# The sums of W_s over q: VectorE and a way through HBM in place of two products with ones

## The chip, the core and the metric

The kernel runs on one core of a Trainium2 chip. The metric is the device time of one execution in microseconds (us), the median of several runs. The core's engines work side by side, each through its own queue, and wait for one another by semaphores: TensorE (PE) multiplies, VectorE (DVE) and ScalarE (ACT) work elementwise, GpSimd (POOL) does small things and issues some transfers, and SyncE (SP) issues most of the transfers.

## What is computed

One layer of an encoder over 1024 positions of 1024 features. Of its parts, the spatial gate matters here:

```python
def spatial_gating(u, v, w_s, b_s, ln_g, ln_b):
    v = layer_norm(v, ln_g, ln_b)
    vc = v.reshape(bsz, s // CHUNK, CHUNK, N_HEADS_A, HEAD_DIM_A)
    mixed = jnp.einsum('hpq,bcqhd->bcphd', w_s, vc) + b_s.T[None, None, :, :, None]
    return u * mixed.reshape(bsz, s, D_A)

h = rms_norm(x, pre_g)
u_a, v_a, g_a, z_b, g_b = jnp.split(h @ w_in, ...)
a = spatial_gating(gelu(u_a), gelu(v_a), w_s, b_s, ln_g, ln_b) * silu(g_a)
b = fourier_mix(z_b, w_f, b_f) * silu(g_b)
x = x + rms_norm(concat([a, b]) @ w_out, post_g)
```

W_s is 128x128 for each of four heads. The layer norm's bias ln_b is constant over positions, so its way through the gate is ln_b times the sum of W_s over q, for each head and each p.

## The kernel before

The x is held transposed, features on partitions. Every product that needs float32 is made of three products of rounded halves (mm3, L75 to L78): high by high, high by low, low by high. A helper split (L68 to L73) makes the two halves of a matrix: a cast on ACT and a subtraction on DVE.

The order of PE's work is written out by hand. First the product for v: seven of eight chunks of positions side by side over the eight blocks of features (L234 to L241), then the eighth (L251 to L253). Meanwhile stats (L152) makes the row norms of x: squares on ACT, a power on POOL (rsqrt, L97), then the 1024 factors go to HBM (r_hbm, L159) and come back broadcast to all partitions as R (L160), both on POOL's queue. v_gelu (L169) and v_norm (L175) turn the product into the normalised v, without ln_g and ln_b. In v_norm an rsqrt on POOL stands between two small operations on DVE, and the norms themselves run on ACT.

Then feature_tile (L388) runs for the twelve tiles of 128 features, in two halves of 512 positions each; with the halves numbered through, after(i) (L458) hangs other work behind half i. Behind half 2 stands gate_bias (L376), then gate_head for the first head (L424), whose products take v and the transposed W_s (ws_sb); the other heads follow behind halves 4, 6 and 8. z_fold, z_step, wz_load and the weights of later tiles (feature_load, which ends in the splits such as wf2h and wf2l) lie between. gate_bias adds ln_b times the row sums of W_s into Tb, which holds b_s broadcast; gate_head reads Tb on DVE only.

Before the change the row sums come from PE. W_s lies transposed in ws_sb, q on partitions, so two products with a matrix of rounded ones, of the high half and of the low half (row_sum, L142 to L144), leave the sums in every partition of a PSUM bank (pt). The split of ws_sb into wss (L384, L385) stands ahead of the feature tiles. The rounded ones (ones_r) are made by ACT as its first operation (L93).

PE, and ACT inside one stretch (L242 to L255), keep the written order; POOL and DVE do so only late, from the last four feature tiles on. Elsewhere a planner orders each engine by its own costs: what is ready and stands first in the program goes first. The planner also hands out the 40 big buffers (slot, L57), and a load waits in SP's queue until its buffer is free.

Of the kernel before, what the change touches and what calls it, by code (L numbers as in the profile page):

```python
# [7 lines left out]
F32 = mybir.dt.float32  # L8
F32R = mybir.dt.float32r
AF = mybir.ActivationFunctionType  # L10
ALU = mybir.AluOpType
PE = mybir.EngineType.PE

P = 128
S = 1024
# [15 lines left out]
def encoder_layer_kernel(  # L31
# [6 lines left out]
    w_fea: bass.AP,  # L38
    w_out: bass.AP,
    w_sT: bass.AP,  # L40
    w_f: bass.AP,
    b_s: bass.AP,
    post_g: bass.AP,
# [3 lines left out]
    nc = tc.nc  # L47

    big = ctx.enter_context(tc.tile_pool(name="big", bufs=1))
    con = ctx.enter_context(tc.tile_pool(name="con", bufs=1))  # L50
# [6 lines left out]
    def slot(name, shape=(P, 1024), dt=F32):  # L57
        return big.tile(list(shape), dt, tag="S", name=name, bufs=NS)
# [6 lines left out]
    def bank(name):  # L65
        return ps.tile([P, 512], F32, tag="ps", name=name)

    def split(src, hi, lo, hi_on_act=True):  # L68
        if hi_on_act:
            nc.scalar.copy(hi, src)  # L70
        else:
            nc.vector.tensor_copy(hi, src)
        nc.vector.tensor_tensor(lo, src, hi.bitcast(F32), op=ALU.subtract)  # L73
# [14 lines left out]
    pre_g, ln_g, b_f, ln_b = (vec_sb[:, a:b] for a, b in ((0, 8), (8, 12), (12, 16), (16, 20)))  # L88

    ones = con.tile([P, P], F32, name="ones")  # L90
    nc.vector.memset(ones, 1.0)
    ones_r = con.tile([P, P], F32R, name="ones_r")
    nc.scalar.copy(ones_r, ones)  # L93
    expo = con.tile([P, 8], F32, name="expo")
    nc.gpsimd.memset(expo, -0.5)

    def rsqrt(dst, src):  # L97
        nc.gpsimd.tensor_tensor(dst, src, expo[:, 0:src.shape[1]], op=ALU.pow)
# [13 lines left out]
    for kt in range(KT):  # L112
# [13 lines left out]
        h = slot(f"hh{kt}", dt=F32R)  # L126
# [12 lines left out]
    def chunk(t, c):  # L139
        return t[:, c * P:(c + 1) * P]  # L140

    def row_sum(o, hi, lo, sl):  # L142
        nc.tensor.matmul(o, ones_r, hi[:, sl], start=True, stop=False)
        nc.tensor.matmul(o, ones_r, lo[:, sl], start=False, stop=True)  # L144


    rcol = con.tile([P, 8], F32, name="rcol")
    msq = con.tile([P, 8], F32, name="msq")
    R = slot("R")
    r_hbm = ctx.enter_context(tc.tile_pool(name="hbm", bufs=1, space=bass.MemoryType.DRAM)).tile([1, S], F32, name="r_hbm")  # L150

    def stats():  # L152
        for c in range(8):
            xc = raw_slot(f"xc{c}")
            nc.sync.dma_start(xc, x[c * P:(c + 1) * P])
            nc.scalar.activation(xc, xc, AF.Square, accum_out=msq[:, c:c + 1])
        nc.vector.tensor_scalar(msq, msq, 1.0 / D, EPS, op0=ALU.mult, op1=ALU.add)
        rsqrt(rcol, msq)
        nc.gpsimd.dma_start(r_hbm.rearrange("o (c p) -> p (o c)", c=8), rcol)  # L159
        nc.gpsimd.dma_start(R, r_hbm.broadcast_to([P, S]))  # L160
# [8 lines left out]
    def v_gelu(c, pv):  # L169
        nc.scalar.activation(v[:, c], pv, AF.Gelu, scale=rcol[:, c:c + 1])  # L170
        nc.vector.bn_stats(vst[:, c], v[:, c])
        nc.vector.bn_aggr(vmv[:, c], vst[:, c])


    def v_norm(c0, c1):  # L175
        nc.vector.tensor_scalar_add(vnb[:, c0:c1], vmv[:, c0:c1, 1], EPS)
        rsqrt(vrs[:, c0:c1], vnb[:, c0:c1])
        nc.vector.scalar_tensor_tensor(vnb[:, c0:c1], vmv[:, c0:c1, 0], -1.0, vrs[:, c0:c1], op0=ALU.mult, op1=ALU.mult)
        for c in range(c0, c1):
            nc.scalar.activation(v[:, c], v[:, c], AF.Identity, scale=vrs[:, c:c + 1], bias=vnb[:, c:c + 1])  # L180

    def v_step(pv, c, kt):
        wh, wl = (t[:, kt % 2] for t in wv[kt // 2])
        mm3(pv, chunk(hh[kt], c), chunk(hl[kt], c), wh, wl, kt == 0, kt == KT - 1)
# [6 lines left out]
    def wz_load(i):  # L191
        wr = raw_slot(f"wz{i}")
        wrv = wr.rearrange("p (k n) -> p k n", k=2)
        nc.sync.dma_start(wrv, w_nat[0, 2 * i:2 * i + 2].rearrange("k p n -> p k n"))
        fw = tmp(f"fw{i}", (P, 2, 512))
        w4 = wrv.rearrange("p k (g c) -> p k g c", g=4)
        e4 = fw[:, :, 0:260].rearrange("p k (g c) -> p k g c", g=4)
        o4 = fw[:, :, 260:512].rearrange("p k (g c) -> p k g c", g=4)
        a, b = w4[:, :, :, 1:64], w4[:, :, :, 127:64:-1]
        nc.vector.tensor_tensor(e4[:, :, :, 1:64], a, b, op=ALU.add)  # L200
        nc.vector.tensor_tensor(o4, a, b, op=ALU.subtract)
        nc.vector.tensor_copy(e4[:, :, :, 0:65:64], w4[:, :, :, 0:65:64])
        for k in range(2):
            kt = 2 * i + k
            h5 = h512[:, kt:kt + 1]
            nc.vector.tensor_tensor(h5, hh[kt].bitcast(F32)[:, 512:513], hl[kt].bitcast(F32)[:, 512:513], op=ALU.add)
            if kt == 0:
                nc.vector.tensor_scalar_mul(acc, fw[:, k, 0:260], h5)
            else:
                nc.vector.scalar_tensor_tensor(acc, fw[:, k, 0:260], h5, acc, op0=ALU.mult, op1=ALU.add)  # L210
        t = slot(f"wzh{i}", (P, 2, 512), F32R), slot(f"wzl{i}", (P, 2, 512), F32R)
        split(fw, *t)
        wz.append(t)

    wsTb = slot("wsTb", (P, 2, 512))
    ws_sb, Tb = wsTb[:, 0], wsTb[:, 1]
# [3 lines left out]
    def const_load():  # L220
        nc.sync.dma_start(ws_sb, w_sT)
        nc.sync.dma_start(Tb, b_s.broadcast_to([P, 512]))
        nc.sync.dma_start(cs_sb, dft[:, 780:909])
        nc.sync.dma_start(wf_sb, w_f)

    def feature_load(f):
        wr = raw_slot(f"wf{f}r")
        nc.sync.dma_start(wr, w_fea[f])
        wh = slot(f"wf{f}h", dt=F32R)
        wl = slot(f"wf{f}l", dt=F32R)  # L230
        split(wr, wh, wl)
        return wh, wl
# [9 lines left out]
    with tc.manual_schedule(engines={mybir.EngineType.Activation}):  # L242
        stats()
        wq = [feature_load(0)]
        wz_load(0)
        const_load()
        for c in range(7):
            v_gelu(c, pvs[c])
        wq.append(feature_load(1))
        v_norm(0, 7)  # L250
        pv = bank("pv7")  # L251
        for kt in range(KT):
            v_step(pv, 7, kt)  # L253
        v_gelu(7, pv)
        v_norm(7, 8)  # L255
# [119 lines left out]

    def gate_bias():  # L376

        pt = bank("pt")
        row_sum(pt, wss[:, 0], wss[:, 1], slice(0, 512))
        for hd in range(4):  # L380
            sl = slice(hd * P, (hd + 1) * P)
            nc.vector.scalar_tensor_tensor(Tb[:, sl], pt[:, sl], ln_b[:, hd:hd + 1], Tb[:, sl], op0=ALU.mult, op1=ALU.add)

    wss = slot("wss", (P, 2, 512), F32R)  # L384
    split(ws_sb, wss[:, 0], wss[:, 1])  # L385


    def feature_tile(f, epilogue):  # L388
# [69 lines left out]
    def after(i):  # L458
        if i == gate_at[0]:
            gate_bias()  # L460
        for kt in range(KT):
            if FOLD_AT[kt] == i:
                z_fold(kt)
        for j in range(2):
            if WZ_AT[j] == i:
                wz_load(2 + j)
        if i in gate_at:
            gate_head(gate_at.index(i))
        if i in z_at:
            kt = z_at.index(i)  # L470
            z_step(kt)
        if i == 9:
            nc.sync.dma_start(dft_sb, dft[:, 0:780])
            channel_split()
        if i == z_at[-1]:
            channel_dft()
            z_evac()
        if i in DFT_AT:
            dft_group(DFT_AT.index(i))
        if i == 22:  # L480
            for _ in range(2):
                next(ahead)
# [198 lines left out]
    lo, hi = slice(0, 512), slice(512, 1024)  # L681
    cuts = (0, 256), (256, 512)
    at = {}
    for n, (g, key) in enumerate(ORDER):
        a, b = 2 * g, 2 * g + 1
        op = ops.pop((g, key))
# [123 lines left out]
```

## Time and profile before

| | us |
|---|---|
| time, median of 3 runs | 311.56 (311.33 to 311.60) |
| the profiled execution | 311.69 |
| its span | 309.6 |
| PE busy | 302.5 (98%) |
| DVE busy | 228.1 (74%) |
| ACT busy | 131.4 (42%) |
| POOL busy | 22.9 (7%) |

The span runs from the first to the last instruction of one profiled execution; the 2.09 us between span and time lie around it. Matmuls are pipelined: a matmul's row shows longer than the step from its start to the next one's start.

### The profile page before, as it was taken

Reading aid. Unit: us, or ns where it says so; the run is one execution under the profiler, and the core shown is the slowest. Engines: PE = TensorE matmul, PEld = TensorE weight load, DVE = VectorE, ACT = ScalarE, POOL = GpSimd, SP = SyncE. Lnnn points to the kernel's source line nnn. Section 1 sums busy time; section 2 is a strip of 40 time slices with the busy share of each in tenths; the row PEclk is TensorE's granted clock in tenths of the full one; section 3 lists DMA queues with packets and bytes.
Section 4 is the critical chain, followed back from the end, with each engine's and each line's share of the span. In section 5 each row is a group of like instructions: output and inputs, shape, how many; then the busy total and the mean of one; then the engine's idle time right before and its main releaser. Section 6 shows DMA issues by size and latency. Waiting matters only on the chain.

```text
span 309.6 us, 3974 instructions
## 1 busy us (share of the span) xinstructions
PE 302.5 (98%) x1497; PEld 254.4 (82%) x1497; DVE 228.1 (74%) x424; ACT 131.4 (42%) x215; POOL 22.9 (7%) x29
## 2 busy tenths in 40 slices
PE   8999999999999999999999999999999999999992
PEld 7888888888888888888888888888888888888881
DVE  4880643579888999987446798655898998898764
ACT  4887376423131333243241334433555554433321
POOL 0000301010000000000000000002300302030210
PEclk9999999999999999999999999999999999999998
DMA  7999715013214252130010107328990163749373
GB/s 252 414 406 409 260 68 177 30 68 128 78 59 147 68 202 56 68 128 10 0 69 2 68 0 233 109 68 243 223 214 1 18 119 67 204 70 276 131 197 144
DMA packets 15427, 42.42 MB, mean 137 GB/s; under 512 B 1456, under 2 KB 1712, under 8 KB 15408
## 3 DMA queue, kind: packets, MB, share of 16 engines
q1 hardware_dynamic: 12880, 35.87, 32.6%
q0 software_dynamic: 2528, 6.30, 11.4%
q8 instruction: 12, 0.20, 0.3%
q14 instruction: 7, 0.06, 0.1%
HBM read 37.96 MB, written 4.20 MB: 136 GB/s over the span
## 4 chain that ended last, share of the span: by engine, by line
PE 98%; DVE 0%; DVEq 0%; POOLq 0%; ACT 0%; issue 0%; ACTq 0%
PE pf L77 14%; PE pf L76 14%; PE pf L78 14%; PE pz L285 7%; PE pv L78 4%; PE pv L77 4%; PE pv L76 4%; PE bb L76 4%; PE bb L78 4%; PE bb L77 4%; PE bc L78 2%; PE bc L77 2%; PE bc L76 2%; PE pg L431 2%; PE ba L76 2%; PE ba L78 2%
## 5 line engine op out<-in xcount | busy, mean ns | idle before, releaser
L446 DVE TENSOR_TENSOR t<-pf,R 128x512 f32<-128x512 f32 x16 | 11.0, 686 | 15.8 <-PE pf L78 15.8
L78 PE MATMUL pv<-wvh,hl 128*128 128x512 f32 x57 | 22.5, 395 | 0.0
L447 ACT ACTIVATE t<-t 128x512 f32<-128x512 f32 x16 | 10.1, 631 | 29.2 <-DVE t L446 29.2
L77 PE MATMUL pv<-wvl,hh 128*128 128x512 f32 x57 | 22.5, 394 | 0.0
L70 ACT CAST fh<-sd 128x1024 fp32r<-128x1024 f32 x8 | 8.4, 1049 | 33.1 <-DVE sd L273 33.1
L76 PE MATMUL pv<-wvh,hh 128*128 128x512 f32 x57 | 22.4, 393 | 0.0
L528 POOL DMA_DIRECT2D wo<-in_w_out x6 | 7.2, 1210 | 175.2 <-PE pf L78 150.3
L285 PE MATMUL pz<-wzh,fh 128*128 128x260 f32 x64 | 18.1, 283 | 0.0
L285 PE MATMUL pz<-wzh,fl 128*128 128x260 f32 x64 | 18.0, 281 | 0.0
L285 PE MATMUL pz<-wzl,fh 128*128 128x260 f32 x64 | 18.0, 281 | 0.0
L562 ACT CAST cq<-s 128x512 fp32r<-128x512 f32 x16 | 9.9, 619 | 17.0 <-DVE s L554 15.3
L644 ACT ACTIVATE jk<-y 128x512 f32<-128x512 f32 x12 | 7.6, 632 | 18.6 <-DVE y L717 7.0
L271 DVE TENSOR_TENSOR sd<-hs 128x384 f32<-128x384 f32 x16 | 14.5, 909 | 0.2
L73 DVE TENSOR_TENSOR fl<-sd,fh 128x1024 fp32r<-128x1024 f32 x8 | 9.8, 1223 | 5.2 <-ACT fh L70 5.1
L77 PEld LDWEIGHTS pv<-wvl,hh 128*128 128x128 f32 x57 | 10.7, 188 | 2.6
L76 PEld LDWEIGHTS pv<-wvh,hh 128*128 128x128 f32 x57 | 10.7, 188 | 2.5
L440 ACT ACTIVATE mixA<-t 128x512 f32<-128x512 f32 x8 | 5.1, 632 | 18.1 <-DVE t L439 18.1
L78 PEld LDWEIGHTS pv<-wvh,hl 128*128 128x128 f32 x57 | 10.7, 187 | 2.5
L439 DVE TENSOR_TENSOR t<-pf,R 128x512 f32<-128x512 f32 x8 | 5.5, 690 | 9.5 <-PE pf L78 9.5
L285 PEld LDWEIGHTS pz<-wzl,fh 128*128 128x128 f32 x64 | 12.1, 189 | 0.3
L285 PEld LDWEIGHTS pz<-wzh,fh 128*128 128x128 f32 x64 | 12.1, 189 | 0.3
L285 PEld LDWEIGHTS pz<-wzh,fl 128*128 128x128 f32 x64 | 12.1, 189 | 0.0
(381 smaller groups left out, 939.5 us busy)
## 6 DMA issues: line engine op xcount, KB each, us to landing
wo<-in_w_out SPq DMA_DIRECT2D x10, 512.0 KB, 4.5
xc<-in_x SPq DMA_DIRECT2D x8, 512.0 KB, 10.0
xr<-in_xT SPq DMA_DIRECT2D x7, 512.0 KB, 7.6
hs<-in_xT SPq DMA_DIRECT2D x7, 512.0 KB, 3.3
wo<-in_w_out POOLq DMA_DIRECT2D x6, 512.0 KB, 9.3
y<-in_x POOLq DMA_DIRECT2D x5, 512.0 KB, 5.2
out<-y SPq DMA_DIRECT2D x5, 512.0 KB, 3.0
wv<-in_w_nat SPq DMA_DIRECT2D x8, 256.0 KB, 6.8
```

What stands on the lines that cost most here:

```text
L70: nc.scalar.copy(hi, src)
L73: nc.vector.tensor_tensor(lo, src, hi.bitcast(F32), op=ALU.subtract)
L76: nc.tensor.matmul(o, lh, rh, start=start, stop=False, **kw)
L77: nc.tensor.matmul(o, lh, rl, start=False, stop=False, **kw)
L78: nc.tensor.matmul(o, ll, rh, start=False, stop=stop, **kw)
L271: nc.vector.tensor_tensor(sd[:, i, 1:4], hv[:, 1:4], hv[:, 7:4:-1, ::-1], op=op)
L285: nc.tensor.matmul(pz[t][:, cs], l[:, i, t], r[:, cs], start=kt == 0 and i == 0 and j == 0, stop=kt == KT - 1 and i == 1 and j == 2, skip_ ...
L446: nc.vector.tensor_tensor(t, pf, R[:, sl], op=ALU.mult)
L447: nc.scalar.activation(t, t, AF.Silu)
L528: nc.gpsimd.dma_start(t, quarter(add, i), accum_op=ALU.add)
L562: nc.scalar.copy(t[:, 0], src)
L644: nc.scalar.activation(jk[:, 0:w], src, AF.Square, accum_out=ssq[c][:, j:j + 1])
```

## The change

W_s comes in a second time in its own order, p on partitions and q along the row, as a new input w_s (128x512, the four heads side by side). It lands in ws_n, one half of a big buffer (wsnr). One tensor_reduce on DVE sums each head's 128 columns into ws_sum (128x4). Its 512 numbers go to HBM (s_hbm) by a transfer on POOL's queue, and a second transfer on POOL's queue broadcasts them to all partitions as ws_row, the other half of the buffer. This is issued behind feature_load(1) and ahead of v_norm(0, 7). gate_bias reads ws_row in place of pt. The two products, the bank pt, the split wss and ones_r are gone.

```diff
     ones = con.tile([P, P], F32, name="ones")
     nc.vector.memset(ones, 1.0)
-    ones_r = con.tile([P, P], F32R, name="ones_r")
-    nc.scalar.copy(ones_r, ones)
...
-    def row_sum(o, hi, lo, sl):
-        nc.tensor.matmul(o, ones_r, hi[:, sl], start=True, stop=False)
-        nc.tensor.matmul(o, ones_r, lo[:, sl], start=False, stop=True)
-
...
         wq.append(feature_load(1))
+
+        wsnr = slot("wsnr", (P, 2, 512))
+        ws_n, ws_row = wsnr[:, 0], wsnr[:, 1]
+        ws_sum = con.tile([P, 4], F32, name="ws_sum")
+        s_hbm = hbm.tile([1, 512], F32, name="s_hbm")
+        nc.sync.dma_start(ws_n, w_s)
+        nc.vector.tensor_reduce(ws_sum, ws_n.rearrange("p (h q) -> p h q", h=4), axis=mybir.AxisListType.X, op=ALU.add)
+        nc.gpsimd.dma_start(s_hbm.rearrange("o (h p) -> p (o h)", h=4), ws_sum)
+        nc.gpsimd.dma_start(ws_row, s_hbm.broadcast_to([P, 512]))
         v_norm(0, 7)
...
     def gate_bias():
 
-        pt = bank("pt")
-        row_sum(pt, wss[:, 0], wss[:, 1], slice(0, 512))
         for hd in range(4):
             sl = slice(hd * P, (hd + 1) * P)
-            nc.vector.scalar_tensor_tensor(Tb[:, sl], pt[:, sl], ln_b[:, hd:hd + 1], Tb[:, sl], op0=ALU.mult, op1=ALU.add)
-
-    wss = slot("wss", (P, 2, 512), F32R)
-    split(ws_sb, wss[:, 0], wss[:, 1])
+            nc.vector.scalar_tensor_tensor(Tb[:, sl], ws_row[:, sl], ln_b[:, hd:hd + 1], Tb[:, sl], op0=ALU.mult, op1=ALU.add)
...
         "w_sT": a["w_s"][0].transpose(2, 0, 1).reshape(128, 512),
+        "w_s": a["w_s"][0].transpose(1, 0, 2).reshape(128, 512),
```

## Rows read from the trace of the kernel before

**Rows 1.** The page: busy us by engine; DVE's busy tenths in 40 slices.

```profile
PE 302.5 (98%) x1497; PEld 254.4 (82%) x1497; DVE 228.1 (74%) x424; ACT 131.4 (42%) x215; POOL 22.9 (7%) x29
...
DVE  4880643579888999987446798655898998898764
```

**Rows 2.** The page: the chain that ended last, share of the span by engine.

```profile
PE 98%; DVE 0%; DVEq 0%; POOLq 0%; ACT 0%; issue 0%; ACTq 0%
```

**Rows 3.** Stretches: length, busy us by engine (PE, PEld, DVE, ACT, POOL), PEclk, DMA.

```profile
77.60:303.70 226.10, 225.96 (x1153) 190.87 (x1151) 180.40 (x335) 85.94 (x151) 16.20 (x18) 1.00 0.39 107
303.70:309.60 5.90, 0.00 (x0) 0.00 (x0) 2.02 (x5) 0.43 (x2) 0.54 (x1) 0.81 0.42 164
```

**Rows 4.** Timeline of PE: start us, us, line, out<-in, count.

```profile
66.93 0.40 PE L143 MATMUL pt<-wss,ones_r 128*128 128x512 f32 x1
...
67.39 1.95 PE L431 MATMUL pg<-wsTb,v 128*128 128x128 f32 x16
...
78.05 0.39 PE L78 MATMUL pf<-hh,wf2l 128*128 128x512 f32 x1
```

**Rows 5.** Timeline of DVE, 59 to 78 us: start, us, operation [idle before, releaser].

```profile
59.19 0.69 DVE L171 BATCH_NORM_STATS2 vst<-v 128x6 f32<-128x512 f32 x1
...
63.42 0.68 DVE L73 TENSOR_TENSOR wss<-wsTb,wss 128x512 fp32r<-128x512 f32 x1
...
70.06 1.13 DVE L382 SCALAR_TENSOR_TENSOR wsTb<-pt,head,wsTb 128x128 f32<-128x128 f32 x4
...
75.55 1.22 DVE L73 TENSOR_TENSOR wf2l<-wf2r,wf2h 128x1024 fp32r<-128x1024 f32 x1
76.68 1.28 DVE L267 SCALAR_TENSOR_TENSOR hs<-hs,head,R 128x1024 f32<-128x1024 f32 x1
```

**Rows 6.** SP's queue: an issue (start, us), and a wait (total, times, longest us).

```profile
48.84 0.33 SPq L266 DMA_DIRECT2D hs<-in_x  x1
...
SPq L266 <- PE pv L77: 17.0, 1, 17.0
```

**Rows 7.** DMA issues: queue, count, KB each, us from issue to landing.

```profile
wsTb<-in_w_sT SPq DMA_DIRECT2D x1, 256.0 KB, 9.6
...
wz<-in_w_nat SPq DMA_DIRECT2D x1, 512.0 KB, 11.7
...
r_hbm<-rcol POOLq DMA_DIRECT2D x1, 4.0 KB, 8.5
...
R<-r_hbm POOLq DMA_DIRECT2D x1, 512.0 KB, 4.0
```

**Rows 8.** Timelines of POOL (three rows) and DVE (the last), 34 to 50 us.

```profile
34.02 1.12 POOL L159 DMA_DIRECT2D r_hbm<-rcol  x1 [0.32 <-POOL rcol L98]
42.78 0.58 POOL L160 DMA_DIRECT2D R<-r_hbm  x1 [7.65 <-DMA r_hbm<-rcol]
47.88 1.51 POOL L98 TENSOR_TENSOR vrs<-vnb,expo 128x7 f32<-128x7 f32 x1 [4.51 <-DVE vnb L176]
...
42.79 1.29 DVE L171 BATCH_NORM_STATS2 vst<-v 128x6 f32<-128x512 f32 x2 [4.70 <-ACT v L170]
```

**Rows 9.** Timeline of ACT: the norms of v, chunks 0 to 6 and 7.

```profile
49.69 5.05 ACT L180 ACTIVATE v<-v,vnb,vrs 128x512 f32<-128x512 f32 x7 [2.53 <-DVE vnb L178]
...
64.81 0.82 ACT L180 ACTIVATE v<-v,vnb,vrs 128x512 f32<-128x512 f32 x1 [1.90 <-DVE vnb L178]
```

**Rows 10.** Timelines of ACT's start and its Gelu table, and PE's first product.

```profile
0.74 1.28 ACT L93 ACT_TABLE_LOAD   x1 [0.74 <-PEq L803]
...
2.94 0.51 ACT L134 ACTIVATE hh<-head 128x256 fp32r<-128x256 f32 x1 [0.61 <-DMA head<-in_x]
...
40.78 1.28 ACT L170 ACT_TABLE_LOAD   x1 [3.94 <-PE pv L78]
...
4.49 1.20 PE L238 MATMUL pv<-wvh,hh 128*128 128x512 f32 x2
```

More of the change, by code (lines that the diff above doesn't have):

```diff
@@ L40, in encoder_layer_kernel @@
     w_sT: bass.AP,
+    w_s: bass.AP,
     w_f: bass.AP,
@@ L149, in encoder_layer_kernel @@
     R = slot("R")
-    r_hbm = ctx.enter_context(tc.tile_pool(name="hbm", bufs=1, space=bass.MemoryType.DRAM)).tile([1, S], F32, name="r_hbm")
+    hbm = ctx.enter_context(tc.tile_pool(name="hbm", bufs=1, space=bass.MemoryType.DRAM))
+    r_hbm = hbm.tile([1, S], F32, name="r_hbm")
     def stats():
```

## Prediction

> **What bounds the kernel now.** I read the page's busy table and slices first, then the chain of waits, then the table by stretches, then TensorE's timeline round the two products that go, and last the engines and queues that the new path will use. The reader is to see in the page [rows 1] that TensorE (PE) is busy 302.5 of 309.6 us and in the chain [rows 2] that 98% of what ended last is PE. The table by stretches [rows 3] makes it sharper: from 77.60 to 303.70 there are 225.96 us of matmuls in 226.10 us, at full granted clock, and the last matmul is followed by a tail of 5.90 us. So PE never waits after its start, and an edit counts by two things alone: how much matmul time it takes away, and whether it makes any operand late. VectorE (DVE) is busy 74% on average, but nine tenths and more in the tenth slice (69.7 to 77.4), right after the edit [rows 1], so an operand from it can easily be late.
>
> The profiled execution took 311.69 us, a span of 309.60 and 2.09 around it. The median shown is 311.56, 0.13 less; I make the sum against 311.69 and take 0.13 off at the end.
>
> **What is removed from PE.** The first of the two products with ones starts at 66.93, and the gate's first product follows them at 67.39 [rows 4]. Starts count, since matmuls overlap: 67.39 - 66.93 = 0.46 us. As nothing but PE is late anywhere behind [rows 2, 3], the whole 0.46 comes off the end. This is the only gain on the path.
>
> **What is removed elsewhere.** The split of the transposed W_s goes: a cast on ScalarE (ACT) and a subtraction of 0.68 us on DVE at 63.42 [rows 5]; also the rounding of ones on ACT at the start. None is on the chain [rows 2], so they are worth nothing to the end; the 0.68 is room for DVE in a stretch where it has little.
>
> **What is added.** One load of 256 KB on SP's queue; one tensor_reduce over 128x512; a write of 512 single floats to HBM and a broadcast of 256 KB back, both on POOL's queue. The four additions into Tb now read SBUF and wait for that broadcast instead of PE.
> - The load stands between those of wf1r and of the second wz in program order. SP was through with wz at 31.8, since the hs load that went at 48.84 had waited 17.0 us by then [rows 6]; so I put the new load at about 31. The load of W_s transposed, as large and in the same stretch, took 9.6 us to land and that wz 11.7 [rows 7]: it lands at 41 to 43. What stands behind it on SP is wz and the hs loads, none of which PE waits for [rows 2], and hs doesn't go before 48.84 for want of a buffer anyway: cost nothing.
> - tensor_reduce isn't in the trace. Its nearest rows are statistics of as many columns, 0.69 us, and a subtraction, 0.68 [rows 5]; from below, half of an operation over 1024 columns of 1.28 [rows 5], 0.64. I take 0.68. DVE stands idle for 4.70 us up to 42.79 [rows 8], and there it costs nothing; at the upper end of its landing it delays the statistics behind it by 0.7 to 1, which the slack worked out below covers. If the planner orders it between 56 and 76 it takes the place of the subtraction that went, 0.68 for 0.68.
> - The write of 512 floats is half of the r_hbm write of 1024, which took 1.12 us of POOL [rows 8] and 8.5 us to land [rows 7]. For the new write I take 8.5 as the upper and the 4.0 of the broadcast R [rows 7] as the lower end, and work with 8.5, because the form is that of r_hbm. POOL is busy with R until 43.36 [rows 8], so the write is issued at 43.4 and has landed at 51.9; ws_row is issued then and lands 4.0 later, at 55.9. The additions run at 70.06 today [rows 5]: 14 us to spare.
> - The four additions take 1.13 us together from PSUM [rows 5]. From SBUF the nearest row is again the 1.28 over 1024 columns: an eighth of it, 0.16 each, from below, and all of it from above would be absurd for 128 columns; the 0.28 each of today is nearest in shape. Not on the path.
>
> The Trainium skill, "DMA: Bandwidth & Descriptors", section "Anatomy of one DMA — SWDGE (gpsimd) path", puts the fixed cost of such a transfer at about 2.0 us. By it the write would land 6.5 us sooner and rival 1 below would keep 2.4 of its 8.9 us of lateness (an estimate from that page); the trace's 8.5 us disagrees and decides.
>
> **What is queued behind the new waits.** On POOL the issue of ws_row waits for the write to land. Behind it, if the planner keeps program order, stands the rsqrt of the norm of v, at 47.88 now [rows 8]; it would run at 51.9 + 0.58 = 52.5. Who waits: the norm of seven chunks on ACT, 5.05 us from 49.69 [rows 9]; then gelu of the eighth chunk, 0.7 like one norm, to 55.4; then its statistics on DVE at 59.19 [rows 5], which leaves 3.8 us of slack; and then the last norm on ACT, which ends at 65.63 [rows 9]. The gate's eighth product needs that at 66.93 + 7 x 0.12 = 67.8 after the change (1.95 us for sixteen, [rows 4]), which leaves 2.1 more. So the rsqrt may be some 5.9 us late, at 53.8, before PE notices, and 52.5 fits. On DVE the additions hold up what follows them in order: wf2l ends at 76.77 [rows 5] and a matmul needs it at 78.05 [rows 4], 1.3 us of slack.
>
> **Buffers.** The raw tile takes one of the 40 big buffers at about 31 instead of the split tile at about 60. The hs load waited 17.0 us for one [rows 6]. If the new load takes the last free buffer, wz goes at 48.84 instead and lands 4.0 later, and hs behind it. PE waits for neither today [rows 2]; I cost it at nothing, and if that cover is gone it is rival 4.
>
> **Sum.** 311.69 - 0.46 = 311.23 for the profiled execution, 311.10 against the median: 0.15% less. About 0.2%, 0.62 us, is what a measurement of this kernel can tell from no change, so the forecast lies within it.
>
> **Rivals.**
> 1. *The detour is late and POOL stands still (slower).* If the load of W_s is the one that gets no buffer, it goes at 48.84, lands 4.0 later at 52.8, is summed at 53.6, the write lands at 62.1, and only then ws_row is issued. If the planner put that issue ahead of the rsqrt, the latter moves from 47.88 to 62.7. ACT norms from 64.5 to 69.5, gelu 0.7, statistics 0.7, rsqrt to norm 1.8 and the norm 0.8 as now [rows 5, 8, 9]: 73.5 instead of the 67.8 at which PE wants it. PE stalls 5.7: 311.56 - 0.46 + 5.7 = 316.8. It decides from an rsqrt later than 53.8. For it: the 17.0 us wait for a buffer and the 8.5 us landing; against it: the load stands ahead of wz and hs in program order, and wz did get a buffer. Chance 0.08.
> 2. *The planner's order shifts on DVE (slower).* DVE's order is the planner's; the additions are free to move ahead and the sum is new. If sum and additions, 0.68 + 1.13, come in front of wf2l, 0.5 of the 1.81 goes beyond its slack and eats the gain: 311.6. If the scaling of hs behind it, 1.28 at 76.68 [rows 5], changes places with it as well, 1.8 of stall: 312.9. I take the middle, 312.3. For it: DVE full there [rows 1] and a slack of 1.3 us; against it: 0.68 went from the same stretch. Chance 0.14.
> 3. *The table load at the start waits.* The first table load of ACT ran at 0.74 with the rounding of ones; it will now belong to the first cast of hh, which waits for its DMA until 2.94 [rows 10]. The load of the Gelu table began only when the wait for PE was over [rows 10]. If so here, 2.94 + 1.28 + 0.51 = 4.73 instead of 3.45, and the first matmul that needs it moves from 4.49 to about 4.8: 0.3 back, 311.4. Against it: the first table load was held by the start alone, not by the memset that its cast needed. Chance 0.10.
> 4. *Nothing comes off.* The 0.46 could be given back in front of some later operand, all of whose slacks I haven't read: 311.6. Chance 0.08.
>
> **How the numbers follow.** Forecast 0.60, rivals 0.08, 0.14, 0.10, 0.08. Predicted is the forecast's 311.1. Its own range is 310.8 to 311.4 (the runs shown differ by 0.27 us). The range to 312.6 takes in rivals 3, 4 and the better half of rival 2, and leaves out 0.15: rival 1 and the worse half. Faster by over 0.2% needs 0.16 us beyond the 0.46: I give it 0.20, from the forecast alone. Within 0.2%: the rest of the forecast, 0.40, and rivals 3 and 4, 0.18, together 0.58. Slower by over 0.2%: rivals 1 and 2, 0.22.
>
> **What would show it.** Right: the gate's first product one matmul step behind the feature tile's last, where three lie now, PE without idle time, and the last matmul 0.46 sooner. The sum on DVE before 44 and ws_row landed before 60 show the detour's step; an rsqrt later than 53.8 or a PE wait at the gate shows rival 1; a PE wait on wf2l rival 2; a table load at 2.9 rival 3. A gain of over 1 us would mean that PE had losses I didn't see.

## The result, and the profile after

The changed kernel takes 318.62 us (median of 5 runs, 318.45 to 318.98) beside 311.60 for the kernel before on the same chip: a ratio of 1.0233, 95% interval 1.0222 to 1.0244, so it is slower by 7.0 us. The prediction was 311.1 with a range to 312.6. The profiled execution took 318.56, with a span of 316.6 against 309.6; the whole loss lies inside the span.

The page of the changed kernel, its busy times, the granted clock of PE in 40 slices and the chain that ended last:

```profile
PE 305.4 (96%) x1495; PEld 256.2 (81%) x1495; DVE 227.9 (72%) x424; ACT 130.9 (41%) x213; POOL 23.9 (8%) x31
...
PEclk9999999999699999999999999999999999999998
...
PE 90%; DMA 4%; DVE 3%; issue 0%; DVEq 0%; POOLq 0%; ACT 0%; ACTq 0%
PE pf L77 12%; PE pf L79 12%; PE pf L78 12%; PE pz L290 8%; PE pv L79 4%; PE pv L78 4%; PE pv L77 4%; PE bb L77 4%; PE bb L78 4%; PE bb L79 3%; DMA s_hbm<-ws_sum 3%; PE bc L77 2%; PE bc L78 2%; PE bc L79 2%; PE ba L78 2%; PE ba L77 2%
```

Beside [rows 1, 2]: PE is busy longer with two products fewer, its clock has a dent in one slice, and DMA and DVE have come into the chain, DMA with the write of the sums (s_hbm<-ws_sum). PE waits in three new places behind the first tile: for v at the gate, and for fh and fl at the first z product. (z_fold scales and folds a block of x and splits it into fh and fl; z_step multiplies these.) PE's timeline, and two rows of the kernel before:

```profile
66.86 1.72 PE L431 MATMUL pg<-wsTb,v 128*128 128x128 f32 x14
69.56 0.49 PE L431 MATMUL pg<-wsTb,v 128*128 128x128 f32 x2 [0.98 <-ACT v L176]
...
78.04 0.59 PE L290 MATMUL pz<-wzh,fh 128*128 128x260 f32 x1 [2.43 <-ACT fh L71]
...
79.41 0.58 PE L290 MATMUL pz<-wzh,fl 128*128 128x260 f32 x1 [0.57 <-DVE fl L74]
...
84.31 0.63 PE L77 MATMUL pf<-hh,wf2h 128*128 128x512 f32 x1
...
85.03 0.40 PE L79 MATMUL pf<-hh,wf2l 128*128 128x512 f32 x1
```

```profile
74.74 0.28 PE L285 MATMUL pz<-wzh,fh 128*128 128x260 f32 x1
...
77.59 0.39 PE L76 MATMUL pf<-hh,wf2h 128*128 128x512 f32 x1
```

The gate starts at 66.86 instead of 67.39 [rows 4]: the two products are gone, as predicted. The first z product, at 74.74 before, starts at 78.04; the third feature tile, at 77.59 before, at 84.31; and its first product with wf2l at 85.03 instead of 78.05 [rows 4]. From there on the lateness stays at 7.0 to the end. The stretches (length; busy us of PE, PEld, DVE, ACT, POOL; granted clock) show that the last part is not waiting alone:

```profile
75.60:78.00 2.40, 0.01 (x1) 0.00 (x0) 2.40 (x7) 1.06 (x2) 0.00 (x0) 1.00 0.09 14
78.00:79.40 1.40, 0.80 (x2) 0.50 (x2) 1.40 (x3) 0.94 (x1) 0.00 (x0) 0.51 0.85 322
79.40:82.00 2.60, 2.59 (x12) 2.59 (x13) 2.60 (x4) 0.63 (x1) 0.00 (x0) 0.50 0.56 224
82.00:84.30 2.30, 2.30 (x12) 2.30 (x12) 2.27 (x3) 0.00 (x0) 0.00 (x0) 0.50 0.00 0
84.30:86.00 1.70, 1.70 (x8) 1.37 (x8) 1.68 (x6) 0.00 (x0) 0.00 (x0) 0.83 0.00 0
```

PE stood idle for 2.4 us and was then granted half its clock, the lower of its two levels, up to 84.3: the 24 products of the first z_step took 6.27 us (78.04 to 84.31) instead of 2.85.

What came late is read off DVE and POOL (start, us; in brackets the idle time before and what ended it), with the fold and an rsqrt of the kernel before behind them:

```profile
56.53 0.68 DVE L252 TENSOR_REDUCE ws_sum<-wsnr 128x4 f32<-128x512 f32 x1
...
68.44 0.16 DVE L174 SCALAR_TENSOR_TENSOR vnb<-vmv,vrs 128x1 f32<-128x1 f32 x1 [5.82 <-POOL vrs L97]
...
71.66 1.14 DVE L385 SCALAR_TENSOR_TENSOR wsTb<-wsnr,head,wsTb 128x128 f32<-128x128 f32 x4 [1.92 <-DMA wsnr<-s_hbm]
72.71 1.28 DVE L272 SCALAR_TENSOR_TENSOR hs<-hs,head,R 128x1024 f32<-128x1024 f32 x1
...
78.14 1.22 DVE L74 TENSOR_TENSOR fl<-sd,fh 128x1024 fp32r<-128x1024 f32 x1
```

```profile
57.51 0.82 POOL L253 DMA_DIRECT2D s_hbm<-ws_sum  x1 [8.19 <-DVE ws_sum L252]
67.26 0.56 POOL L254 DMA_DIRECT2D wsnr<-s_hbm  x1 [8.93 <-DMA s_hbm<-ws_sum]
67.83 0.58 POOL L97 TENSOR_TENSOR vrs<-vnb,expo 128x1 f32<-128x1 f32 x1
```

```profile
63.59 0.94 POOL L98 TENSOR_TENSOR vrs<-vnb,expo 128x1 f32<-128x1 f32 x1 [14.19 <-DVE vnb L176]
...
64.63 1.28 DVE L267 SCALAR_TENSOR_TENSOR hs<-hs,head,R 128x1024 f32<-128x1024 f32 x1
```

The transfers (queue, KB, us from issue to landing):

```profile
wsnr<-in_w_s SPq DMA_DIRECT2D x1, 256.0 KB, 10.3
wsnr<-s_hbm POOLq DMA_DIRECT2D x1, 256.0 KB, 4.4
...
s_hbm<-ws_sum POOLq DMA_DIRECT2D x1, 2.0 KB, 9.5
```

W_s has landed by 40.8 (issued at 30.48, 10.3 to land), but the planner put the sum behind DVE's first work on a feature tile, at 56.53. The write and the spread (the broadcast of the sums to all partitions) take 9.5 and 4.4 us, until 71.7. The additions (L385), which stood at 70.06 behind the fold of x [rows 5], now stand ahead of it, and DVE does nothing else while it waits for the spread; the fold, at 64.63 before, starts at 72.71. A second wait hangs on the same write: the rsqrt of the eighth chunk of v (chunk 7 where the count starts at 0) stands behind the issue of the spread on POOL and runs at 67.83 instead of 63.59. DVE waits in order for this one too: of the 8.1 us by which the fold is late, it stood 5.82 for the rsqrt and 1.92 for the spread.

By starts on PE, the loss adds up as follows.

| | us |
|---|---|
| two products gone (gate 67.39 to 66.86) | -0.53 |
| gate to first z product (7.35 to 11.18): waits for v and fh | +3.83 |
| z_step (2.85 to 6.27): wait for fl and slow clock | +3.42 |
| first two products of the third tile (0.46 to 0.72): slow clock | +0.26 |
| sum, 78.05 to 85.03 | +6.98 |

### The profile page after: what moved, and what is told of

It reads as the page before. It is cut to its first block, busy times and chain, and to the rows that moved or that the text cites. A ratio compares the mean times of both kernels' runs of the same rounds, so it can differ in the third digit from the quotient of the medians.

```text
span 316.6 us, 3968 instructions
## 1 busy us (share of the span) xinstructions
PE 305.4 (96%) x1495; PEld 256.2 (81%) x1495; DVE 227.9 (72%) x424; ACT 130.9 (41%) x213; POOL 23.9 (8%) x31
## 2 busy tenths in 40 slices
DMA packets 15682, 42.93 MB, mean 136 GB/s; under 512 B 1520, under 2 KB 1776, under 8 KB 15664
## 3 DMA queue, kind: packets, MB, share of 16 engines
q0 software_dynamic: 2640, 6.56, 11.7%
## 4 chain that ended last, share of the span: by engine, by line
PE 90%; DMA 4%; DVE 3%; issue 0%; DVEq 0%; POOLq 0%; ACT 0%; ACTq 0%
PE pf L77 12%; PE pf L79 12%; PE pf L78 12%; PE pz L290 8%; PE pv L79 4%; PE pv L78 4%; PE pv L77 4%; PE bb L77 4%; PE bb L78 4%; PE bb L79 3%; DMA s_hbm<-ws_sum 3%; PE bc L77 2%; PE bc L78 2%; PE bc L79 2%; PE ba L78 2%; PE ba L77 2%
## 5 line engine op out<-in xcount | busy, mean ns | idle before, releaser
L290 PE MATMUL pz<-wzh,fh 128*128 128x260 f32 x64 | 19.3, 302 | 2.4 <-ACT fh L71 2.4
L290 PE MATMUL pz<-wzh,fl 128*128 128x260 f32 x64 | 19.2, 299 | 0.6 <-DVE fl L74 0.6
L290 PE MATMUL pz<-wzl,fh 128*128 128x260 f32 x64 | 19.1, 298 | 0.0
L290 PEld LDWEIGHTS pz<-wzh,fh 128*128 128x128 f32 x64 | 13.1, 205 | 3.1 <-ACT fh L71 2.9
L290 PEld LDWEIGHTS pz<-wzh,fl 128*128 128x128 f32 x64 | 13.2, 206 | 0.9 <-DVE fl L74 0.9
L290 PEld LDWEIGHTS pz<-wzl,fh 128*128 128x128 f32 x64 | 13.2, 206 | 0.3
L439 DVE TENSOR_TENSOR t<-pf,R 128x512 f32<-128x512 f32 x8 | 5.5, 690 | 10.3 <-PE pf L79 10.3
```

Of the source, the lines that this page charges most:

```text
L290: nc.tensor.matmul(pz[t][:, cs], l[:, i, t], r[:, cs], start=kt == 0 and i == 0 and j == 0, stop=kt == KT - 1 and i == 1 and j == 2, skip_ ...
```

## The experiments

The leading theory (A) was that the time is set by the additions, which wait on DVE for the detour and hold up the fold behind them; the rivals, that POOL's wait and the late rsqrt set it (B), that buffers and loads moved back by one place do (C), or that the detour costs as such wherever it stands (D). All times beside the kernel before, at 311.55 to 311.58 us in these comparisons. Diffs are against the changed kernel; line numbers shift a little from kernel to kernel.

**No sums at all.** The whole block of W_s and the additions are left out (the term of ln_b is then missing from the gate).

```diff
-        wsnr = slot("wsnr", (P, 2, 512))
...
-        nc.gpsimd.dma_start(ws_row, s_hbm.broadcast_to([P, 512]))
...
-            nc.vector.scalar_tensor_tensor(Tb[:, sl], ws_row[:, sl], ...)
```

> Leaves out the sums of W_s and their four additions altogether (Tb stays b_s): no load, no detour, no products with ones, all else as after the change. It prices the term that the prediction took off, 0.46 us for the two products. If that is all the products cost, 0.9985 of before (311.1 us) with the gate's first product one matmul step behind the tile's last, and PE without idle time. If the rest of PE's work gives it back somewhere, 1.000.

Measured: 310.75 us, ratio 0.9974 (0.9965 to 0.9984), and PE has no new wait except 0.2 us at the start. So all that the two products, their split and the additions could give back is 0.5 to 1.1 us, and the 7.0 (7.9 beside this run) come with the detour and the additions that wait for it.

**The detour without the additions.** Load, sum, write and spread stay; the four additions are left out.

```diff
-            nc.vector.scalar_tensor_tensor(Tb[:, sl], ws_row[:, sl], ...)
+        pass
```

> As after the change, with load, sum and both POOL transfers, but the four additions into Tb are left out (Tb stays b_s), so nothing on DVE waits for ws_row. Theory A (the additions wait for a late ws_row and hold up the first fold behind them on DVE; that makes TensorE wait at the first z_step and run it at half clock): the wait at the gate stays, 1.2 us, the first fold starts 3 us sooner and is in time: about 312.5 us. Theory B (the rsqrt of the eighth chunk, stuck behind the issue of ws_row on POOL, is what makes all late): 316 to 318, since POOL's order is the same. Theory C (the buffers and loads that moved back by one place make operands late): 318.

Measured: 313.49 us, ratio 1.0060 (1.0046 to 1.0075). Waits of PE, then DVE's wait for the rsqrt and its fold:

```profile
PE pg L429 <- ACT v L176: 1.3, 1, 1.3
...
PE pz L290 <- DVE fl L74: 0.6, 1, 0.6
```

```profile
68.44 0.16 DVE L174 SCALAR_TENSOR_TENSOR vnb<-vmv,vrs 128x1 f32<-128x1 f32 x1 [6.09 <-POOL vrs L97]
...
69.65 1.28 DVE L272 SCALAR_TENSOR_TENSOR hs<-hs,head,R 128x1024 f32<-128x1024 f32 x1
```

POOL's rows are as in the changed kernel (rsqrt again at 67.83). The fold comes 3.1 us sooner, the wait for fh and the slow clock are gone, and with them 5.1 of the 7.0 us. That is theory A's mechanism, with 1.0 us more left over than it had. What remains over the run without sums, 2.7 us, is for the most part POOL's share: the wait for v at the gate, and DVE's 6.09 us for the same rsqrt, which keep the fold 5 us behind its place before the change. This execution also has 0.4 us of waiting for wvh at its start, which belongs to neither.

**The rsqrt ahead of the spread.** POOL's order is written by hand in the stretch: the rsqrt of the eighth chunk goes ahead of the issue of the spread (and, in the program, that of the first seven ahead of the write, where POOL had it anyway). The order on DVE, ACT and PE is the same.

```diff
-    with tc.manual_schedule(engines={mybir.EngineType.Activation}):
+    with tc.manual_schedule(engines={mybir.EngineType.Activation, mybir.EngineType.Pool}):
...
+        v_norm(0, 7)
         nc.gpsimd.dma_start(s_hbm.rearrange("o (h p) -> p (o h)", h=4), ws_sum)
-        nc.gpsimd.dma_start(ws_row, s_hbm.broadcast_to([P, 512]))
-        v_norm(0, 7)
...
         v_norm(7, 8)
+        nc.gpsimd.dma_start(ws_row, s_hbm.broadcast_to([P, 512]))
```

> As after the change, but POOL keeps the written order in that stretch, and the issue of ws_row is written behind the norm of the eighth chunk: the rsqrt is no longer behind the wait for the write. Theory A: the wait at the gate goes, but ws_row lands at 71.6 as before, the additions and the fold behind them are as late, and TensorE waits longer at the first z_step by what it gained: 318 us, no better. Theory B: 311.5 to 313. Theory C: 318, with TensorE waits elsewhere than at the fold.

Measured: 318.72 us, ratio 1.0224 (1.0205 to 1.0243): no gain. POOL, DVE, and PE's waits:

```profile
62.21 0.75 POOL L97 TENSOR_TENSOR vrs<-vnb,expo 128x1 f32<-128x1 f32 x1 [4.00 <-DVE vnb L172]
67.24 0.60 POOL L260 DMA_DIRECT2D wsnr<-s_hbm  x1 [4.29 <-DMA s_hbm<-ws_sum]
```

```profile
71.97 1.14 DVE L385 SCALAR_TENSOR_TENSOR wsTb<-wsnr,head,wsTb 128x128 f32<-128x128 f32 x4 [7.68 <-DMA wsnr<-s_hbm]
```

```profile
PE pz L290 <- ACT fh L71: 4.0, 1, 4.0
```

The wait at the gate is gone, and the one at fh has grown from 2.4 to 4.0. DVE stands still as long as before, 7.68 us for the spread alone instead of 5.82 for the rsqrt and 1.92 for the spread. Two late chains run side by side; mending the one that ends first changes nothing. POOL's late rsqrt isn't what sets the 318.6.

**PE kept busy in its wait.** Eleven products into a bank that nothing reads fill the idle 2.4 us.

```diff
             if kt == 0:
+                busy = bank("busy")
+                for _ in range(11):
+                    nc.tensor.matmul(busy, chunk(hh[0], 0), hh[0][:, 0:512], start=True, stop=True)
```

> The changed kernel, with 11 more products of 128x512 ahead of the first z product, into a bank that nothing reads; they take about 11 x 0.23 = 2.5 us at full clock, the length of TensorE's wait there (75.60 to 78.04). The operands come no earlier. Theory E (the wait itself is only part of the loss, the rest is the clock of 0.50 that the chip grants after it): the clock stays at 1.00, the first z products still start near 78.1, wait for fl until 79.4, and then run in some 2.6 us; the second tile's third half starts near 82.0 instead of 84.3, and the time is 316.0 us (315.4 to 316.6). Theory F (late operands alone make up the loss; the slow products are waits that the profile doesn't show): 318.6 us, no change from the changed kernel.

Measured: 316.33 us, ratio 1.0149 (1.0134 to 1.0165): 2.3 us less than the changed kernel, by doing more work. PE's timeline, and two stretches behind the wait:

```profile
74.99 2.69 PE L474 MATMUL busy<-hh 128*128 128x512 f32 x11
78.02 0.39 PE L290 MATMUL pz<-wzh,fh 128*128 128x260 f32 x1 [0.33 <-ACT fh L71]
...
79.39 0.39 PE L290 MATMUL pz<-wzh,fl 128*128 128x260 f32 x1 [0.87 <-DVE fl L74]
...
82.08 0.39 PE L77 MATMUL pf<-hh,wf2h 128*128 128x512 f32 x1
```

```profile
78.00:80.00 2.00, 1.12 (x7) 0.91 (x8) 2.00 (x4) 0.91 (x1) 0.00 (x0) 1.00 0.90 330
80.00:82.00 2.00, 2.00 (x20) 2.00 (x19) 2.00 (x3) 0.63 (x1) 0.00 (x0) 1.00 0.47 184
```

The operands come at the same times (78.02 and 79.39) and the clock stays at 1.00. Theory E holds (what it calls the second tile's third half is the first half of the third feature tile, at 82.08): of the 3.42 us of z_step in the table, 2.21 were the clock (84.31 to 82.08, all but 0.02) and 1.21 the wait for fl.

**The detour early, beside R.** The whole change with its block moved: W_s is loaded ahead of x, summed among the row statistics, its write goes right behind that of r_hbm, the spread right behind R; POOL keeps the written order.

```diff
     def stats():
+        nc.sync.dma_start(ws_n, w_s)
...
+        nc.vector.tensor_reduce(ws_sum, ...)
...
+        nc.gpsimd.dma_start(s_hbm.rearrange("o (h p) -> p (o h)", h=4), ws_sum)
...
+        nc.gpsimd.dma_start(ws_row, s_hbm.broadcast_to([P, 512]))
```

> All of the change, with the detour moved forward: W_s is loaded ahead of the eight loads for the row norms, summed before the row norms' rsqrt, and its write is issued on POOL right behind that of r_hbm, so that both writes are waited for at once; ws_row is issued behind R; POOL keeps the written order in that stretch. Theories A and B: ws_row lands at about 48, nobody waits, and the two products' 0.46 us come off: 311.1 us, faster than before by 0.15%. Theory C (the tile in the buffer from even earlier on): above 313.

Measured: 310.75 us, ratio 0.9977 (0.9968 to 0.9985), the time of the run without any sums, and faster than both kernels. PE has no new wait. DVE and POOL:

```profile
52.88 0.35 DVE L386 SCALAR_TENSOR_TENSOR wsTb<-wsnr,head,wsTb 128x128 f32<-128x128 f32 x1 [5.36 <-DMA wsnr<-s_hbm]
...
53.73 1.54 POOL L97 TENSOR_TENSOR vrs<-vnb,expo 128x7 f32<-128x7 f32 x1 [4.66 <-DVE vnb L182]
```

The same instructions and transfers, started 21 us sooner (the write at 36.16), cost nothing, so the detour doesn't cost as such. It isn't that nobody waits, as expected: the write takes 11.7 us here, the planner again moves additions up, DVE stands 5.36 us for the spread, and the rsqrt of chunks 0 to 6 runs 5.9 us later than before the change. All of it fits into slack, and the fold starts at 64.51. What counts is where a wait falls.

**The sum where the prediction had it.** Only the place of the block in the program changes: ahead of the seven v_gelu instead of behind feature_load(1). The planner then sets the sum among DVE's statistics.

```diff
         const_load()
+        wsnr = slot("wsnr", (P, 2, 512))
...
+        nc.gpsimd.dma_start(ws_row, s_hbm.broadcast_to([P, 512]))
         for c in range(7):
             v_gelu(c, pvs[c])
```

> The whole change, and the computation whole; only its block (load of W_s, sum, the two transfers) stands in the program ahead of the normalisation of the first seven chunks instead of behind it. The planner then puts the sum among DVE's statistics, where the prediction had it, and GpSimd's queue holds R, the write of the sums, rsqrt of chunks 0 to 6, the spread, rsqrt of chunk 7. Theory A (the time is set by when the sum is issued, by way of the additions that stand ahead of DVE's first fold): sum near 46, write landed near 56, spread landed near 60, additions done by 63, first fold no later than 66, TensorE without a wait ahead of the first z product: 310.8 to 311.5 us. Theory D (this detour costs wherever it stands, since GpSimd stands still in it and DVE waits for it): rsqrt or the additions hold up the next tile, TensorE waits over 1 us near 67 to 78 again and its clock falls: 314 us or more.

Measured: 316.89 us, ratio 1.0169 (1.0139 to 1.0200). Theory A's number was missed by 5 us; the number is theory D's, but the run before this one rules out its "wherever it stands". DVE, and PE's new waits of 0.5 us and more, in an execution of 315.22 us:

```profile
47.04 0.67 DVE L248 TENSOR_REDUCE ws_sum<-wsnr 128x4 f32<-128x512 f32 x1
...
63.09 0.88 DVE L385 SCALAR_TENSOR_TENSOR wsTb<-wsnr,head,wsTb 128x128 f32<-128x128 f32 x3 [5.51 <-DMA wsnr<-s_hbm]
...
65.33 0.69 DVE L167 BATCH_NORM_STATS2 vst<-v 128x6 f32<-128x512 f32 x1
```

```profile
PE pg L431 <- ACT v L176: 1.7, 1, 1.7
...
PE pf L77 <- ACT wf2h L71: 0.5, 1, 0.5
PE pf L79 <- DVE wf2l L74: 0.5, 1, 0.5
```

The sum came 9.5 us sooner, and the planner moved three additions up as well, ahead of the statistics of the eighth chunk (65.33 here, 58.65 in the changed kernel). DVE again stood still for the spread, now for 5.5 us, and a different chain came late. The executions with a mean clock of 0.996 and 0.999 took 315.22 and 314.89, those with 0.984 to 0.992 took 316.81 to 318.23. That points to the clock for part of the loss here too, but only the execution of 315.22 has a trace, and there the clock stayed at 1.00 behind all these waits. So an earlier sum doesn't mend the kernel while the additions keep the planner's place.

**The write in runs of 16 bytes.** The four sums of a partition go side by side to HBM, in 128 runs, instead of 512 single floats. The row then holds the sums in another order, so Tb gets sums of other columns.

```diff
-        nc.gpsimd.dma_start(s_hbm.rearrange("o (h p) -> p (o h)", h=4), ws_sum)
+        nc.gpsimd.dma_start(s_hbm.rearrange("o (p h) -> p (o h)", h=4), ws_sum)
```

> The changed kernel with one edit: each partition's four sums go to HBM side by side, 128 runs of 16 bytes, instead of 512 single floats at a distance of 512 bytes. The row that is read back then holds the sums in another order, so the additions to Tb take sums of other columns; all instructions and their durations are the same. Theory G (the 9.5 us of the write are the price of 512 single-float pieces): it lands in 2 to 4 us, the spread is issued near 61, the additions stand near 66, the first fold stands near 67 instead of 72.7, and the time is 311 to 312.5 us. Theory H (9.5 us is what this queue takes for any write that goes to HBM and is waited for): still 9 to 10 us, and 318.6 us.

Measured: 310.86 us, ratio 0.9980 (0.9969 to 0.9991). The write lands in 1.7 us instead of 9.5:

```profile
s_hbm<-ws_sum POOLq DMA_DIRECT2D x1, 2.0 KB, 1.7
```

PE, DVE, ACT and POOL have the order of the changed kernel throughout, and the buffers and loads are the same, so nothing but this landing differs: theory C is out. Theory G holds: one line takes back the whole loss and leaves the gain. Whether the price lies in the number of pieces, their size or their distance isn't separated here.

**The same with the right columns.** The additions read every fourth column of the row, and the whole computation is there.

```diff
+        nc.gpsimd.dma_start(s_hbm.rearrange("o (p h) -> p (o h)", h=4), ws_sum)
...
-            nc.vector.scalar_tensor_tensor(Tb[:, sl], ws_row[:, sl], ...)
+            nc.vector.scalar_tensor_tensor(Tb[:, sl], ws_row[:, hd:512:4], ...)
```

> The whole change and the whole computation, with the write in 128 runs of 16 bytes and the additions reading every fourth column of the row, so that each sum meets its own column. The order of all engines is that of the changed kernel: the sum still stands at 56.5. Theory G (the landing of the single floats is what tips the change): write landed in under 2 us, additions near 64.5 to 66, no wait of TensorE after the start, 310.9 us (310.5 to 311.4), the time of the run with the same write and the sums in another order; the strided reading adds at most some tenths of a us on DVE. Theory I (the early place of the sum is needed as well): over 312 us.

Measured: 311.03 us, ratio 0.9985 (0.9974 to 0.9995), faster than the kernel before by 0.05% to 0.26%. PE, DVE, ACT and POOL have the order of the changed kernel. POOL and DVE:

```profile
57.46 0.60 POOL L253 DMA_DIRECT2D s_hbm<-ws_sum  x1 [8.19 <-DVE ws_sum L252]
59.49 0.56 POOL L254 DMA_DIRECT2D wsnr<-s_hbm  x1 [1.43 <-DMA s_hbm<-ws_sum]
62.26 0.75 POOL L97 TENSOR_TENSOR vrs<-vnb,expo 128x1 f32<-128x1 f32 x1 [2.22 <-DVE vnb L172]
```

```profile
56.48 0.68 DVE L252 TENSOR_REDUCE ws_sum<-wsnr 128x4 f32<-128x512 f32 x1
...
64.26 1.48 DVE L385 SCALAR_TENSOR_TENSOR wsTb<-wsnr,head,wsTb 128x128 f32<-128x128 f32 x4
65.66 1.27 DVE L272 SCALAR_TENSOR_TENSOR hs<-hs,head,R 128x1024 f32<-128x1024 f32 x1
```

The sum still stands at 56.48, the additions start without a wait, the fold comes 1 us later than before the change and PE doesn't notice. The strided reading costs 0.34 us over four additions.

**The early sum with the write in runs.** The two edits of the last kernel in the kernel with the sum among the statistics.

> The kernel with the sum among the statistics, where three additions had waited for the spread ahead of the second load of DFT rows; only the write is in runs of 16 bytes and the additions read every fourth column. The order of all engines is unchanged. Theory J (that kernel lost its time because the planner set the additions at a place for which the write had to land in far less than 10 us): spread issued near 50.5, landed near 55, additions at 57.6 without a wait, rsqrt of chunk 7 near 61, 310.8 us (310.4 to 311.4), a gain of 6 us over the same order with single floats. Theory K (it lost its time by its order on DVE alone): 314 us or more.

Measured: 312.35 us, ratio 1.0023 (1.0012 to 1.0035), between the two theories. DVE's wait shrank from 5.51 to 0.86 us, and 4.5 of the 6.1 us over the run without sums came back. The write landed in 4.7 us here (10.0 as single floats in the same order), not in 1.7, and POOL waited for it before the spread:

```profile
53.30 0.60 POOL L250 DMA_DIRECT2D wsnr<-s_hbm  x1 [2.88 <-DMA s_hbm<-ws_sum]
```

The spread went at 53.30, nearly 3 us later than J had it. The DMA engines were busy for 0.91 of the stretch from 48.30 to 53.30, with the loads of hs and wf2r in it, and for 0.02 of that from 57.60 to 59.70 in the kernel with 1.7; that this traffic made the difference is likely, not shown. The rest of the time stays with that order: PE waits 0.4 for wf2l and 0.3 for wf3l, and 0.6 at the very start, which the edit doesn't explain. So J names the larger part; the rest is K's order and a write that came later than J had it.

## Why the prediction was wrong

**Right.** PE gained what it was to gain: from the feature tile's last product to the gate's first it is 0.24 us (66.62 to 66.86) instead of 0.70, the 0.46 predicted; the other 0.07 of the table's 0.53 lies ahead of the edit. The kernels in which nothing is late take 310.75 to 311.03. The load was issued at 30.48 and landed at 40.8 (31 and 41 to 43). The sum took 0.68 as priced, the write 9.5 (8.5), the spread 4.4 (4.0). The second wz had to wait for a buffer, until 45.98, and as costed nobody waited for it. The table load stayed at 0.74, so rival 3 is out.

**The step that failed: one timetable for two places.** The prediction allowed the sum two places, DVE's idle stretch before 42.79 and "between 56 and 76", and priced the second as "0.68 for 0.68". That is DVE's time alone. The timetable of the detour, "issued at 43.4", "14 us to spare", was worked out for the first place only. The planner took the second, at 56.53. With the prediction's own durations the spread then lands at 57.2 + 8.5 + 4.0 = 69.7, and the additions stood at 70.06 [rows 5]: of the 14 us to spare 0.4 was left. It landed at 71.7, since the write and the spread took 1.4 us more than priced and each went some 0.3 us after what it waited for. Each duration was near; the start was never set to the other place that the same text allowed. What this lateness alone, with the additions still behind the fold, would have cost, no run shows.

**The second step: "not on the path".** The additions were taken to stay at 70.06, behind the fold. But before the change they couldn't start ahead of the two products at 66.93 [rows 4], and the change took away just that. The planner then put them ahead of the fold in the changed kernel and ahead of the eighth chunk's statistics in the kernel with the earlier sum. In both DVE waited in order for the spread; without the additions the fold came 3.1 us sooner and the time fell by 5.1 us. The same place is harmless once the write lands in 1.7 us (311.03): it costs only together with the late landing. This step weighs more than the first. In the kernel with the sum at the first place the spread landed at 63.1 (58.25 and 4.8), 7 us ahead of the 70.06, and still 5.3 us were lost, because the additions didn't stand at 70.06. That the planner reckons with a much shorter landing than 9.5 us would explain both, and the order that works once the write lands in 1.7 us; its reckoning can't be read from a trace, so this is argued, not shown.

**The third: what is behind the wait on POOL.** The prediction followed the rsqrt of chunks 0 to 6, which ran at 47.81 and didn't stand behind the spread. With the sum late it is the rsqrt of the eighth chunk that does. PE waits 1.0 us for it at the gate, hidden behind the fold's lateness (no gain from mending it alone); once the additions are out of the way it costs most of the 2.7 us that remain.

**The clock.** No term of the sum had it. By the table and the run with a busy PE, 2.21 + 0.26 = 2.5 of the 7.0 us are the granted clock behind the idle 2.4 us; the run itself came out 2.3 us faster.

**The rivals.** Rival 1 came near in size (316.8), but that is luck: it had a late load of W_s hold up the rsqrt of chunks 0 to 6 and PE stall 5.7 us at the gate. Here W_s landed in time, that rsqrt ran as before, and the wait at the gate, its sign, came but was 1.0. Its idea, a late detour with something queued behind it on POOL, was right, its place wrong. Its tipping point, an rsqrt later than 53.8, was reached but not passed: with the detour beside R that rsqrt ran at 53.73 and PE waited for nothing, so nearly all of the 5.9 us of slack was used without harm. Rival 2 had the additions moving ahead on DVE, but ahead of wf2l and at the price of their own 1.81 us, not of their wait. Rival 4 is out: where nothing is late, the 0.46 stays off (311.03).

**The write.** The 9.5 us against 1.7 show why r_hbm, a write of the same form, was the right row to price it by, and that the form is the price. The Trainium skill, "DMA: Bandwidth & Descriptors", section "Rules for kernel authors", says that a non-contiguous last dimension becomes one descriptor per element and should be rearranged to be contiguous. The runs with 16-byte pieces bear out the advice, by 7.8 us of landing at the late place and 5.3 at the early one; the page of the profile counts 15682 packets with either form, so descriptors are not seen. The Trainium skill, "DMA: Bandwidth & Descriptors", section "Anatomy of one DMA — SWDGE (gpsimd) path", gives about 2.0 us as the fixed cost of such a transfer, which the prediction set aside. The 1.7 us of the write in runs are near it, the 4.7 at the early place and the 9.5 us of the single floats are not.

## What to carry to other kernels

When an operation that a planner places may stand in two places, work out the whole chain behind it from each, not only its own engine's time; the later place sets the slack. When a product is removed, ask what it was holding back: its consumer may move ahead of something that matters and wait there, in order, for a transfer. A wait in order costs nothing by itself, as the detour beside R shows; ask what stands behind it and when that is needed. And try small writes to HBM in runs of a partition's own numbers, with the reordering done where they are read: here two lines, from +2.3% to -0.15%.

## What the runs showed of the hardware

- A write of 2 KB from 128 partitions landed in 9.5 us as 512 single floats (9.6 to 11.7 in other kernels here) and in 1.7 us as 128 runs of 16 bytes, on the same queue at the same place. At an earlier place, beside other transfers, it took 10.0 and 4.7. r_hbm, 1024 single floats, took 8.5 us before the change [rows 7] and 9.1 to 13.4 in the kernels after it, hardly longer than half as many.
- After 2.4 us without a matmul PE was granted 0.50 of its clock for the next 6.3 us and 0.83 in the 1.7 us after; after waits of 1.3 and 0.6 us, in the kernel without the additions, and of 1.7 us, in the kernel with the sum among the statistics, it stayed at 1.00. Filling the 2.4 us with useless products saved 2.3 us.
- The additions took 1.14 us for four from SBUF, 1.13 from PSUM [rows 5], and 1.48 with every fourth column read.
